# Latents ahead of the context between an HGRN2 and an RG-LRU layer, with the last adaLN block in that gap

## The chip, the cores and the metric

The kernel runs on one core of one Trainium2 chip. The metric is the device time of one execution in microseconds (us), as the median of several runs. The engines are named as the profile names them: PE is TensorE (PEld its weight loads), DVE is VectorE, ACT is ScalarE, POOL is GpSimd, and SP is the queue that issues the transfers of the weights.

## The reference

A backbone of two layers on 512 latent tokens with a prefix of 256 context tokens, 1024 channels. Layer 0 is an HGRN2 mixer (gated linear attention, 16 heads of 128), layer 1 an RG-LRU mixer (convolution of width 4, then a gated recurrence). Cut to the lines that matter here:

```
def reference(x, c, ctx, c_ctx, ada_w, ada_b, norm_g, ...):
    sc = jax.nn.silu(c)
    scc = jax.nn.silu(c_ctx)
    for i in range(DEPTH):
        shift, scale, gate = jnp.split(sc @ ada_w[i] + ada_b[i], 3, axis=-1)
        shift_c, scale_c, gate_c = jnp.split(scc @ ada_w[i] + ada_b[i], 3, axis=-1)
        h = (_rms(x, norm_g[i]) * (1.0 + scale[:, None]) + shift[:, None]).astype(x.dtype)
        hc = (_rms(ctx, norm_g[i]) * (1.0 + scale_c) + shift_c).astype(ctx.dtype)
        ...
            yc, y = hgrn2_mixer(hc, h, hg_w_in[j], lb_all[i], hg_norm_g[j], hg_w_out[j], need_ctx)
        ...
            yc, y = rglru_mixer(hc, h, rg_w_in[j], rg_conv_w[j], rg_conv_b[j], rg_w_a[j], rg_b_a[j], ...)
        x = (x + gate[:, None] * y).astype(x.dtype)
        if need_ctx:
            ctx = (ctx + gate_c * yc).astype(ctx.dtype)
    return _rms(x, final_norm_g).astype(x.dtype)
```

All is float32 to its full precision. [...]

## The kernel before

Channels lie on the 128 partitions, tokens along the free dimension: columns 0 to 255 are the context (segment 0), 256 to 767 the latents (segment 1). The residual stream is one tile `x1` of 8 blocks of 128 channels.

**Products.** `mm3` (L307) issues three matmuls per pair: high by high (L311), high by low of the moving side (L312), low weights by high (L313). A weight tile of 128x1024 comes by a transfer on SP's queue (L114), and `wget` has it split: ACT copies the high part `hi` (L129), DVE subtracts to get `lo` (L130). The raw, `hi` and `lo` tiles rotate through three buffers each, unless `W.slots` gives a weight other tiles.

**The end of layer 0.** `out_item` (L391) multiplies a head's result by its output weights into eight blocks for each segment, tiles `o15_d_i` for the last head, d the block, i the segment; DVE adds each block, times the gate, to `x1` (L405). For head 15, `out_item` does first the context's eight blocks and then the latents' eight, and `sumsq` squares each block as it comes: ACT squares (L285 the first of a group, L288 the others), and the squares are added into three tiles `acc1_0..2` (L289) by POOL for blocks 1 to 3, by DVE for blocks 5 and 6, while block 7 is alone.

**The norm between the layers.** `rstd_of` (L255) sums those tiles over the partitions with matmuls of one column (`msh`, L262), takes a root on ACT (L265) and a reciprocal on DVE (L266), and spreads the result over all partitions with matmuls by an identity (`rbh`, L272), once for each segment.

**The start of layer 1.** `hchunk` (L296) makes one block of `h` for one segment: DVE scales (`scr`, L300), ACT adds the shift and rounds to `h_hi` (L304), DVE forms the rest `h_lo` (L305). Behind each block the first products go: `rc0`, `rc1` (context, 256 columns) and `rl0` to `rl2` (latents, 512 columns) for three weight tiles of the input projection; all context blocks come before the latents' in the code. Then `conv` (L776) evaluates the convolution into `xb` (ACT L789, DVE L792), and `rin(0, 1, 1)` makes the second gate half (tile `r`).

**adaLN.** `ada_block(l, b)` (L224) makes one block of shift, scale or gate: four quarters, each a weight tile and four matmuls with 256 columns (L230), a copy `blk` (L236), four small matmuls that transpose it (`adat`, L240), two additions (L245). Block (1, 5), the last, holds a part of layer 1's gate and is not used in the norm. In `extra(h)` each block of layer 1 is a side generator of a head from 10 to 15; the last one runs in the stretch where heads 14 and 15 are worked on, one quarter beside each second level of the scores (`lv`), `adat` between two products of the input projection.

**Order.** The Tile framework's list scheduler sets the order of the instructions of each engine at compile time, from the order of the code, priorities and its own cost figures; on the chip each engine runs its list in order and waits on semaphores.

## Time and profile before

| what | value |
|---|---|
| time, median of 3 runs | 1581.88 us (1580.87 to 1582.18) |
| the profiled execution's own time | 1581.96 us |
| its span | 1580.2 us |
| PE busy | 1531.5 us, 97% of the span |
| DVE busy | 1207.8 us, 76% |
| ACT busy | 902.6 us, 57% |
| POOL busy | 12.7 us, 1% |

The span is what the profiler shows from the first to the last instruction; the time has 1.8 us around it. PE is busy almost all the time, so the page's totals say little about the place that is changed: some 60 us between the last score products of layer 0 and the steady part of layer 1, from about 1075 to 1133 us. In this stretch PE waits and its granted clock falls.

### The profile page before, as it was taken

Reading aid. Unit: us, or ns where it says so; the run is one execution under the profiler, and the core shown is the slowest. Engines: PE = TensorE matmul, PEld = TensorE weight load, DVE = VectorE, ACT = ScalarE, POOL = GpSimd, SP = SyncE. Lnnn points to the kernel's source line nnn. Section 1 sums busy time; section 2 is a strip of 40 time slices with the busy share of each in tenths; the row PEclk is TensorE's granted clock in tenths of the full one; section 3 lists DMA queues with packets and bytes.
Section 4 is the critical chain, followed back from the end, with each engine's and each line's share of the span. In section 5 each row is a group of like instructions: output and inputs, shape, how many; then the busy total and the mean of one; then the engine's idle time right before and its main releaser. Section 6 shows DMA issues by size and latency. Waiting matters only on the chain.

```text
span 1580.2 us, 34022 instructions
## 1 busy us (share of the span) xinstructions
PE 1531.5 (97%) x14740; PEld 1431.9 (91%) x14740; DVE 1207.8 (76%) x1867; ACT 902.6 (57%) x1423; POOL 12.7 (1%) x16
## 2 busy tenths in 40 slices
PE   5999999999999999999999999998999999999995
PEld 3899999999999999999999999987889988988984
DVE  4767678768867868867876786787768887797888
ACT  4554555555554554554545555654577577667874
POOL 0000000000000000000000000001000000000001
PEclk8999999999999999999999999998999999999996
DMA  8231311110211211223232132202212213222111
GB/s 324 84 121 55 95 55 41 55 55 28 82 41 42 68 41 55 81 68 95 68 95 82 55 108 68 95 15 67 67 54 81 83 51 94 80 77 70 55 53 54
DMA packets 33861, 116.80 MB, mean 74 GB/s; under 512 B 3632, under 2 KB 6064, under 8 KB 33712
## 3 DMA queue, kind: packets, MB, share of 16 engines
q1 hardware_dynamic: 32192, 113.26, 23.0%
q8 instruction: 116, 1.90, 0.5%
q10 hardware_dynamic: 1520, 1.37, 0.3%
q14 instruction: 33, 0.27, 0.1%
HBM read 112.52 MB, written 2.10 MB: 73 GB/s over the span
## 4 chain that ended last, share of the span: by engine, by line
PE 93%; DVE 3%; ACT 2%; issue 1%; POOL 1%; DMA 0%; POOLq 0%; ACTq 0%; DVEq 0%
PE in L311 12%; PE in L312 11%; PE in L313 11%; PE v L381 9%; PE lv L460 4%; PE r L313 4%; PE r L312 4%; PE r L311 4%; PE o L565 4%; PE gt L311 3%; PE gt L312 3%; PE gt L313 3%; PE o L311 3%; PE o L313 3%; PE o L312 3%; PE U L533 2%
## 5 line engine op out<-in xcount | busy, mean ns | idle before, releaser
L311 PE MATMUL in<-h_hi,hi 128*128 128x384 f32 x1024 | 350.6, 343 | 3.4 <-ACT h_hi L304 2.7
L312 PE MATMUL in<-h_lo,hi 128*128 128x384 f32 x1024 | 345.8, 338 | 0.3 <-DVE h_lo L305 0.3
L313 PE MATMUL in<-h_hi,lo 128*128 128x384 f32 x1024 | 344.9, 337 | 0.0
L130 DVE TENSOR_TENSOR lo<-raw,hi 128x1024 fp32r<-128x1024 f32 x160 | 195.2, 1220 | 88.1 <-ACT hi L129 84.7
L129 ACT ACTIVATE hi<-raw 128x1024 fp32r<-128x1024 f32 x160 | 168.2, 1057 | 121.3 <-PE in L312 48.7
L311 PEld LDWEIGHTS in<-h_hi,hi 128*128 128x128 f32 x1024 | 193.1, 189 | 16.8 <-issue 9.9
L312 PEld LDWEIGHTS in<-h_lo,hi 128*128 128x128 f32 x1024 | 193.1, 189 | 2.8 <-issue 1.6
L313 PEld LDWEIGHTS in<-h_hi,lo 128*128 128x128 f32 x1024 | 192.8, 189 | 1.2 <-issue 0.8
L509 DVE TENSOR_TENSOR QQ<-QQ,T 128x768 f32<-128x768 f32 x112 | 117.8, 1052 | 20.8 <-ACT qt L491 20.5
L416 ACT ACTIVATE kt<-KK 128x768 f32<-128x768 f32 x112 | 102.4, 915 | 41.1 <-DVE KK L502 32.7
L502 DVE TENSOR_TENSOR KK<-KK,T 128x768 f32<-128x768 f32 x112 | 117.6, 1050 | 9.7 <-ACT kt L416 8.2
L313 PE MATMUL r<-h_hi,lo 128*128 128x512 f32 (+1 forms) x344 | 123.4, 359 | 0.3 <-DVE lo L130 0.3
L312 PE MATMUL r<-h_lo,hi 128*128 128x512 f32 (+1 forms) x344 | 123.1, 358 | 0.0
L311 PE MATMUL r<-h_hi,hi 128*128 128x512 f32 (+1 forms) x344 | 122.9, 357 | 0.0
L337 ACT ACTIVATE sg<-in 128x384 f32<-128x384 f32 x128 | 61.5, 482 | 99.9 <-PE in L313 99.7
L381 PE MATMUL v<-hi,h_hi 128*128 128x256 f32 x384 | 111.3, 290 | 0.0
L381 PE MATMUL v<-hi,h_lo 128*128 128x256 f32 x384 | 107.4, 280 | 0.0
L381 PE MATMUL v<-lo,h_hi 128*128 128x256 f32 x384 | 107.3, 279 | 0.0
L588 DVE RECIPROCAL sq<-sq 128x384 f32<-128x384 f32 x30 | 76.3, 2545 | 21.1 <-ACT sq L582 20.9
L405 DVE SCALAR_TENSOR_TENSOR x<-o,ada,x 128x256 f32<-128x256 f32 (+1 forms) x184 | 82.3, 488 | 11.3 <-PE o L313 10.6
L311 PE MATMUL o<-rhi,hi 128*128 128x384 f32 (+2 forms) x240 | 85.0, 356 | 1.5 <-DVE lo L130 1.2
L313 PE MATMUL gt<-xh,lo 128*128 128x384 f32 x256 | 86.0, 336 | 0.0
(207 smaller groups left out, 3284.4 us busy)
## 6 DMA issues: line engine op xcount, KB each, us to landing
raw<-in_hgw_dram SPq DMA_DIRECT2D x64, 512.0 KB, 3.7
raw<-in_ada_dram SPq DMA_DIRECT2D x48, 512.0 KB, 4.2
raw<-in_rgi_dram SPq DMA_DIRECT2D x32, 512.0 KB, 3.6
raw<-in_hgv_dram SPq DMA_DIRECT2D x16, 512.0 KB, 3.6
raw<-in_hgo_dram SPq DMA_DIRECT2D x16, 512.0 KB, 3.6
raw<-in_rgg_dram SPq DMA_DIRECT2D x16, 512.0 KB, 3.6
raw<-in_rgo_dram SPq DMA_DIRECT2D x16, 512.0 KB, 3.6
x<-in_x_dram SPq DMA_DIRECT2D x8, 384.0 KB, 5.9
```

Of the source, the lines that this page charges most:

```text
L129: self.nc.scalar.activation(hi, r, AF.Copy)
L130: self.nc.vector.tensor_tensor(lo, r, hi.bitcast(F32), ALU.subtract)
L311: PE.matmul(ps, lhsT=wh, rhs=xh, start=first and i == 0, stop=False, skip_group_check=skip)
L312: PE.matmul(ps, lhsT=wh, rhs=xl, start=False, stop=False, skip_group_check=skip)
L313: PE.matmul(ps, lhsT=wl, rhs=xh, start=False, stop=last and i == n - 1, skip_group_check=skip)
L381: PE.matmul(ps, lhsT=xh[:, kk, t], rhs=w[:, k], start=part == 0 and k == 0 and i == 0 and c % 2 == 0, stop=part == 1 and k == 3 and i == 2 ...
L405: V.scalar_tensor_tensor(xs, ps[:, a - c.start:b - c.start], gate[:, d, 1 - j:2 - j], xs, ALU.mult, ALU.add)
L416: A.activation(view(kt, 0, [[2 * B, n], [B, 2], [1, B]]), view(KK, 0, [[2 * B, n], [NT + B, 2], [1, B]]), AF.Copy)
L460: PE.matmul(ps[w * g:w * g + w, w * c:w * c + w], lhsT=kt[:, o:o + w], rhs=rhs, start=c == 0, stop=c == NC - 1, skip_group_check=True, til ...
L502: V.tensor_tensor(kv, kv, view(T, 1, [[2, n], [m - 1, 2], [0, B]]), ALU.mult)
L509: V.tensor_tensor(qv, qv, view(T, m + 1, [[2, n], [-m - 1, 2], [0, B]]), ALU.mult)
L588: V.reciprocal(rs, rs)
```

## The change

The order between the layers is turned round: the latents' eight output blocks, their norm and their `h` and products come first; the context's output blocks (`out_last(k, 0)`) are written one behind each latent block's products, then come the context's norm, `h` and products. Block (1, 5) of adaLN leaves the head loop; its four quarters go ahead of the latents' norm in the code and its rest (`between`) into the norm, and its weights get tiles of layer 0 that are free by then (`wide`). The first gate half's weights, `rin(0, 1, 0)`, also get two such tiles. `h`'s scratch tile rotates through the pool `ktp` (three buffers) in place of two fixed tiles. `conv` takes the latents first, and for `j = 0` without raised priority.

```
-    def out_item(heads, accs=None, done=None):
+    def out_item(heads):
...
-        parts = segs if accs else halves
-        order = [(d, i) for d in range(DK) for i in range(2)]
-        for d, i in sorted(order, key=lambda x: x[1]) if accs else order:
+        for d, i in [(d, i) for d in range(DK) for i in range(2)]:
...
-            if accs:
-                sumsq(accs, THREE, lambda n: ktp.tile([P, NT], F32, name=n, tag="kt"), d, c)
-                if d == DK - 1:
-                    done(i)
...
+    for j in range(4):
+        W.slots["ada", 1, 5, j] = wide[(0, 1, 5, 1)[j]]
+    W.slots["rin", 0, 1, 0] = (wide[0], wide[1])
...
-        return [ada_block(1, h - 10)] if h >= 10 else []
+        return [ada_block(1, h - 10)] if 10 <= h < NH - 1 else []
...
+    def norm1(i, between=()):
         c = segs[i]
-        rs1.extend(rstd_of([chunks(a, c) for a in accs1], ones_d, f"h1_{i}", ((c.stop - c.start) // P,)))
-
-    run_all(out_item((NH - 1,), accs1, norm1))
+        rs1[i], = rstd_of([chunks(a, c) for a in accs1], ones_d, f"h1_{i}", ((c.stop - c.start) // P,), between)
+    w15 = wget("out", NH - 1)
+
+    def out_last(d, i):
+        e, c = slice(P * d, P * d + P), segs[i]
+        ps = dtile(f"o{NH - 1}_{d}_{i}")[:, :c.stop - c.start]
+        mm3(ps, [(w15[0][:, e], w15[1][:, e], st[NH - 1]["r"][0][:, c], st[NH - 1]["r"][1][:, c])])
+        V.scalar_tensor_tensor(x1[:, d, c], ps, ada[0][:, 2, d, 1 - i:2 - i], x1[:, d, c], ALU.mult, ALU.add)
+        sumsq(accs1, THREE, lambda n: ktp.tile([P, NT], F32, name=n, tag="kt"), d, c)
+
+    for d in range(DK):
+        out_last(d, 1)
+    side = ada_block(1, 5)
+    for _ in range(4):
+        next(side)
+    norm1(1, side)
...
-    first = [[(w, dtile(f"rc{e}")[:, :CTX]) for e, w in enumerate(wx)]]
     wg = wget("rin", 0, 1, 0)
...
-    for i, c in enumerate(segs):
+    first = {1: [(w, (dtile if e < 2 else atile)(f"rl{e}")) for e, w in enumerate(wx + [wg])]}
+    for i in (1, 0):
+        c = segs[i]
         for k in range(DK):
-            hchunk(1, k, i, rs1[i], scr[k % 2])
+            hchunk(1, k, i, rs1[i], ktp.tile([P, NT], F32, name=f"scr1_{i}_{k}", tag="kt"))
             for w, ps in first[i]:
                 mm3(ps, hpairs(w, c, [k]), first=k == 0, last=k == DK - 1)
+            if i:
+                out_last(k, 0)
+        if i:
+            norm1(0)
+            first[0] = [(w, dtile(f"rc{e}")[:, :CTX]) for e, w in enumerate(wx)]
...
-        urgent.enter_context(tc.high_priority(400))
+        if j:
+            urgent.enter_context(tc.high_priority(400))
...
-    for i in range(2):
+    for i in (1, 0):
         for e in range(2):
-            conv(0, e, i, first[i][e][1])
+            conv(0, e, i, first[i][e][1], 0)
```

The list of PE at the latents' norm, before. `msh1_1` is the latents' sum, `rc0` and `rc1` the context's products, `rbh1_1_0` the spread result; a row is line, operation, output<-inputs, size.

```order
L313 MATMUL o15_7_1_13016<-rhi15_12761,lo143_12473 128x512
L262 MATMUL msh1_1_13022<-cst_78,acc1_0_12884 128x1 x4
L311 MATMUL rc0_13051<-h_hi_94,hi144_12889 128x256
L262 MATMUL msh1_1_13022<-cst_78,acc1_1_12885 128x1 x4
L262 MATMUL msh1_1_13022<-cst_78,acc1_2_12886 128x1 x4
L311 MATMUL rc1_13052<-h_hi_94,hi145_13045 128x256
L312 MATMUL rc0_13051<-h_lo_95,hi144_12889 128x256
L313 MATMUL rc0_13051<-h_hi_94,lo144_12890 128x256
L312 MATMUL rc1_13052<-h_lo_95,hi145_13045 128x256
L313 MATMUL rc1_13052<-h_hi_94,lo145_13046 128x256
L311 MATMUL rc0_13051<-h_hi_94,hi144_12889 128x256
L311 MATMUL rc1_13052<-h_hi_94,hi145_13045 128x256
```

The latents' norm stands in a row with the context's products here, which begin ahead of its second sum.

The list of PE at the latents' norm, in the changed kernel, from the last matmul of the latents' outputs to the first of the context's.

```order
L313 MATMUL o15_7_1_12907<-rhi15_12727,lo139_12439 128x512
L262 MATMUL msh1_1_12944<-cst_78,acc1_0_12850 128x1 x4
L240 MATMUL adat1_5_12960<-cst_78,blk1_5_12942 128x2 x4
L262 MATMUL msh1_1_12944<-cst_78,acc1_1_12851 128x1 x4
L262 MATMUL msh1_1_12944<-cst_78,acc1_2_12852 128x1 x4
L272 MATMUL rbh1_1_0_12967<-cst_78,rh1_1_12957 128x128 x4
L311 MATMUL rl0_12986<-h_hi_94,hi144_12934 128x512
L311 MATMUL rl1_12987<-h_hi_94,hi145_12974 128x512
L311 MATMUL rl2_12988<-h_hi_94,hi146_12980 128x512
L311 MATMUL o15_0_0_13002<-rhi15_12727,hi139_12438 128x256
L312 MATMUL rl0_12986<-h_lo_95,hi144_12934 128x512
```

Between the sums now stands `adat` of the adaLN block, and no dense product until `rl0`.

The list of DVE behind the reciprocal of the latents' norm, before.

```order
L266 RECIPROCAL rh1_1_13035<-rh1_1_13035 128x4
L305 SCALAR_TENSOR_TENSOR h_lo_95<-scr1_1_13063,ada1_97,h_hi_94 128x256
L300 SCALAR_TENSOR_TENSOR scr1_0_13062<-x1_81,amul_98,rbh1_0_0_12961 128x256
L300 SCALAR_TENSOR_TENSOR scr1_1_13063<-x1_81,amul_98,rbh1_0_0_12961 128x256
L305 SCALAR_TENSOR_TENSOR h_lo_95<-scr1_0_13062,ada1_97,h_hi_94 128x256
L300 SCALAR_TENSOR_TENSOR scr1_0_13062<-x1_81,amul_98,rbh1_1_0_13038 128x512
L305 SCALAR_TENSOR_TENSOR h_lo_95<-scr1_1_13063,ada1_97,h_hi_94 128x256
L300 SCALAR_TENSOR_TENSOR scr1_0_13062<-x1_81,amul_98,rbh1_0_0_12961 128x256
L300 SCALAR_TENSOR_TENSOR scr1_1_13063<-x1_81,amul_98,rbh1_0_0_12961 128x256
L305 SCALAR_TENSOR_TENSOR h_lo_95<-scr1_0_13062,ada1_97,h_hi_94 128x512
L300 SCALAR_TENSOR_TENSOR scr1_1_13063<-x1_81,amul_98,rbh1_1_0_13038 128x512
L305 SCALAR_TENSOR_TENSOR h_lo_95<-scr1_0_13062,ada1_97,h_hi_94 128x256
```

The blocks of both segments alternate here, and no update of `x1` stands among them.

The list of DVE behind the same reciprocal, in the changed kernel (L735 is the update of `x1` in `out_last`).

```order
L266 RECIPROCAL rh1_1_12957<-rh1_1_12957 128x4
L300 SCALAR_TENSOR_TENSOR scr1_1_0_12989<-x1_81,amul_98,rbh1_1_0_12967 128x512
L300 SCALAR_TENSOR_TENSOR scr1_1_1_13008<-x1_81,amul_98,rbh1_1_0_12967 128x512
L305 SCALAR_TENSOR_TENSOR h_lo_95<-scr1_1_0_12989,ada1_97,h_hi_94 128x512
L305 SCALAR_TENSOR_TENSOR h_lo_95<-scr1_1_1_13008,ada1_97,h_hi_94 128x512
L130 TENSOR_TENSOR lo150_13373<-raw150_13345,hi150_13372 128x1024
L735 SCALAR_TENSOR_TENSOR x1_81<-o15_0_0_13002,ada0_96,x1_81 128x256
L735 SCALAR_TENSOR_TENSOR x1_81<-o15_1_0_13021,ada0_96,x1_81 128x256
L735 SCALAR_TENSOR_TENSOR x1_81<-o15_2_0_13042,ada0_96,x1_81 128x256
L300 SCALAR_TENSOR_TENSOR scr1_1_2_13029<-x1_81,amul_98,rbh1_1_0_12967 128x512
L300 SCALAR_TENSOR_TENSOR scr1_1_3_13050<-x1_81,amul_98,rbh1_1_0_12967 128x512
L735 SCALAR_TENSOR_TENSOR x1_81<-o15_3_0_13063,ada0_96,x1_81 128x256
```

The updates of `x1` for the context's blocks now stand among the latents' blocks: three of them ahead of the third `scr`.

The list of DVE at the end of the latents' blocks, in the changed kernel (L810 is the convolution, L792 before).

```order
L300 SCALAR_TENSOR_TENSOR scr1_1_7_13132<-x1_81,amul_98,rbh1_1_0_12967 128x512
L289 TENSOR_TENSOR acc1_1_12851<-acc1_1_12851,sq6_0_13129 128x256
L130 TENSOR_TENSOR lo147_13307<-raw147_12978,hi147_13306 128x1024
L305 SCALAR_TENSOR_TENSOR h_lo_95<-scr1_1_7_13132,ada1_97,h_hi_94 128x512
L266 RECIPROCAL rh1_0_13158<-rh1_0_13158 128x2
L810 SCALAR_TENSOR_TENSOR xb0_13280<-rl0_12986,prm_76,xb0_13280 128x511
L300 SCALAR_TENSOR_TENSOR scr1_0_0_13166<-x1_81,amul_98,rbh1_0_0_13161 128x256
L300 SCALAR_TENSOR_TENSOR scr1_0_1_13176<-x1_81,amul_98,rbh1_0_0_13161 128x256
L300 SCALAR_TENSOR_TENSOR scr1_0_2_13186<-x1_81,amul_98,rbh1_0_0_13161 128x256
L810 SCALAR_TENSOR_TENSOR xb0_13280<-rl0_12986,prm_76,xb0_13280 128x510
L810 SCALAR_TENSOR_TENSOR xb0_13280<-rl1_12987,prm_76,xb0_13280 128x511
L305 SCALAR_TENSOR_TENSOR h_lo_95<-scr1_0_0_13166,ada1_97,h_hi_94 128x256
```

The context's `scr` and `h_lo` rows come behind the latents' last `h_lo`, with rows of the convolution among them.

## Rows read from the trace of the kernel before

**Rows 1.** The page: first line, and shares of the chain that ended last.

```profile
span 1580.2 us, 34022 instructions
...
PE 93%; DVE 3%; ACT 2%; issue 1%; POOL 1%; DMA 0%; POOLq 0%; ACTq 0%; DVEq 0%
```

**Rows 2.** PE's timeline in head 14: start us, us, engine, line, operation, tiles, count.

```profile
995.63 0.39 PE L230 MATMUL ada<-raw,sc 128*32 128x256 f32 x1
996.22 0.44 PE L311 MATMUL in<-h_hi,hi 128*128 128x384 f32 x1
...
1021.09 0.95 PE L240 MATMUL adat<-cst,blk 128*128 128x2 f32 x8
1021.90 0.42 PE L311 MATMUL in<-h_hi,hi 128*128 128x384 f32 x1
```

**Rows 3.** Windows: length, busy PE, PEld, DVE, ACT, POOL; PEclk, DMA, GB/s.

```profile
1020.00:1030.00 10.00, 10.00 (x63) 10.00 (x62) 9.82 (x15) 6.31 (x8) 0.00 (x0) 1.00 0.19 54
1030.00:1040.00 10.00, 7.85 (x180) 6.56 (x182) 9.95 (x13) 6.89 (x9) 0.00 (x0) 1.00 0.15 50
1076.42:1081.42 5.00, 3.79 (x16) 3.38 (x17) 5.00 (x9) 3.19 (x6) 0.29 (x1) 0.66 0.65 202
1075.42:1133.37 57.95, 50.19 (x242) 42.42 (x241) 47.09 (x78) 31.82 (x53) 7.75 (x6) 0.88 0.21 64
1095.00:1100.00 5.00, 5.00 (x26) 5.00 (x25) 3.19 (x6) 1.02 (x2) 0.00 (x0) 0.50 0.40 129
1105.00:1110.00 5.00, 5.00 (x33) 4.59 (x33) 5.00 (x12) 3.42 (x7) 0.00 (x0) 0.97 0.02 3
```

**Rows 4.** PE's timeline; in brackets the idle time before a row and its releaser.

```profile
1036.85 0.63 PE L460 MATMUL lv<-qt,kt 128*32 128x32 f32 x48 [1.55 <-ACT qt L416]
...
1075.25 0.34 PE L313 MATMUL o<-r,lo 128*128 128x384 f32 x1
1094.78 1.68 PE L262 MATMUL msh<-cst,acc 128*128 128x1 f32 x8 [3.29 <-POOL acc L289]
1108.40 0.28 PE L311 MATMUL rc<-h_hi,hi 128*128 128x256 f32 x1
1108.51 0.28 PE L312 MATMUL rc<-h_lo,hi 128*128 128x256 f32 x1
1133.14 0.40 PE L313 MATMUL r<-h_hi,lo 128*128 128x512 f32 x1
1133.37 0.52 PE L311 MATMUL gt<-xh,hi 128*128 128x384 f32 x2
```

**Rows 5.** The chain between the layers: start us, us, engine, tile, line, count.

```profile
1087.60 0.80 PE msh L262 x8
1096.88 3.21 PE msh L262 x16
1101.79 1.71 PE rbh L272 x8
```

**Rows 6.** Timelines of ACT, POOL and DVE between the layers.

```profile
1085.84 1.06 ACT L129 ACTIVATE hi<-raw 128x1024 fp32r<-128x1024 f32 x1 [1.37 <-DMA raw<-in_rgg_dram]
1104.32 0.72 ACT L304 ACTIVATE h_hi<-scr,ada 128x512 fp32r<-128x512 f32 x1 [2.01 <-DVE scr L300]
...
1089.80 1.30 POOL L289 TENSOR_TENSOR acc<-acc,sq 128x512 f32<-128x512 f32 x1 [5.53 <-ACT sq L288]
...
1078.11 1.12 DVE L604 TENSOR_TENSOR rlo<-gs,rhi 128x512 fp32r<-128x512 f32 x1
1095.59 0.68 DVE L289 TENSOR_TENSOR acc<-acc,sq 128x512 f32<-128x512 f32 x1
1103.53 0.75 DVE L300 SCALAR_TENSOR_TENSOR scr<-x,amul,rbh 128x512 f32<-128x512 f32 x1 [1.11 <-PE rbh L272]
1107.49 0.87 DVE L300 SCALAR_TENSOR_TENSOR scr<-x,amul,rbh 128x256 f32<-128x256 f32 x2
1128.00 4.03 DVE L792 SCALAR_TENSOR_TENSOR xb<-rl,prm,xb 128x511 f32<-128x511 f32 x6
```

More of the change, by code (lines that the diff above doesn't have):

```diff
@@ L389, in v_item @@
                 yield 1300.0
-    def out_item(heads, accs=None, done=None):
+    def out_item(heads):
         ws = [wget("out", h) for h in heads]
         gate = ada[0][:, 2]
-        parts = segs if accs else halves
-        order = [(d, i) for d in range(DK) for i in range(2)]
-        for d, i in sorted(order, key=lambda x: x[1]) if accs else order:
+        for d, i in [(d, i) for d in range(DK) for i in range(2)]:
             e = slice(P * d, P * d + P)
-            c = parts[i]
+            c = halves[i]
             ps = dtile(f"o{heads[0]}_{d}_{i}")[:, :c.stop - c.start]
@@ L723, in build @@
              for i, (pl, t, n) in enumerate(((kdp, "kd", NT), (qp, "q", NT), (sp, "S", 2 * (NC - 1) * P)))]
-    rs1 = []
-    def norm1(i):
+    rs1 = {}
+    def norm1(i, between=()):
         c = segs[i]
-        rs1.extend(rstd_of([chunks(a, c) for a in accs1], ones_d, f"h1_{i}", ((c.stop - c.start) // P,)))
-    run_all(out_item((NH - 1,), accs1, norm1))
+        rs1[i], = rstd_of([chunks(a, c) for a in accs1], ones_d, f"h1_{i}", ((c.stop - c.start) // P,), between)
[12 more added lines that the diff above has]
+    norm1(1, side)
     W.presplit = False
     wx = [wget("rin", 0, 0, e) for e in range(2)]
-    first = [[(w, dtile(f"rc{e}")[:, :CTX]) for e, w in enumerate(wx)]]
     wg = wget("rin", 0, 1, 0)
-    first.append([(w, (dtile if e < 2 else atile)(f"rl{e}")) for e, w in enumerate(wx + [wg])])
-    scr = [ktp.tile([P, NT], F32, name=f"scr1_{k}", tag="kt") for k in range(2)]
-    for i, c in enumerate(segs):
+    first = {1: [(w, (dtile if e < 2 else atile)(f"rl{e}")) for e, w in enumerate(wx + [wg])]}
+    for i in (1, 0):
+        c = segs[i]
         for k in range(DK):
-            hchunk(1, k, i, rs1[i], scr[k % 2])
+            hchunk(1, k, i, rs1[i], ktp.tile([P, NT], F32, name=f"scr1_{i}_{k}", tag="kt"))
             for w, ps in first[i]:
                 mm3(ps, hpairs(w, c, [k]), first=k == 0, last=k == DK - 1)
+            if i:
[3 more added lines that the diff above has]
+            first[0] = [(w, dtile(f"rc{e}")[:, :CTX]) for e, w in enumerate(wx)]
     W.presplit = True
@@ L774, in g_evac, with conv @@
         V.tensor_tensor(s["gs"][:, e], ps, s["gs"][:, e], ALU.mult)
-    def conv(j, e, i, ps):
+    def conv(j, e, i, ps, last=1):
         s = rt[j]
@@ L792, in conv @@
             V.scalar_tensor_tensor(dst, src, cw[:, tap:tap + 1], dst, ALU.mult, ALU.add)
-        if i == 1:
+        if i == last:
             A.activation(s["xh"][:, e], xb, AF.Copy)
```

## The prediction

> **What bounds the kernel now.** I read the page first: the span is 1580.2 us and 93% of the chain that ended last is PE's own work [rows 1]. So the kernel is bound by PE, and the change can only act where PE does not work at its full pace. It touches two such places. I looked at both in tables of windows, which give each engine's busy time in a stretch and the granted clock.
>
> In heads 14 and 15 PE is full in some windows, but from 1020 to 1040 it is DVE that has 9.82 and 9.95 of each 10 us, while PE sinks to 7.85 [rows 3]. Work taken from PE is worth its length in the first sort of window, and little in the second.
>
> Between the layers the stretch from 1075.42, where PE is done with the last output matmul of heads 12 to 14 (a step of 0.17 behind its start, [rows 4]), to 1133.37, where layer 1's first `gt` matmul starts [rows 4], takes 57.95 us, with PE busy for 50.19 of it and a mean granted clock of 0.88 [rows 3]. The matmuls in it need far less at full pace. One step from matmul to matmul is 0.23 us for 512 columns and 0.115 for 256 [rows 4]. Head 15's outputs (24 of each size) are 8.4 us, `rc` (48 of 256) 5.6, `rl` (72 of 512) 16.8, the second gate half `r` (24 of 512) 5.6, and the small matmuls of the two norms some 4.9 by the full-pace step of 0.1 us each (0.80 for x8, [rows 5]). That is 41.3 us, so 16.6 are lost, 7.8 by standing still and the rest by the clock: PE waits 3.29 us for POOL's sums, then the small sums take 1.68 for x8, twice as long as 0.80 before [rows 4, 5], and the window at 1095 shows 0.50, the lower level of 1.2 GHz, although PE counts as busy for all of it [rows 3]. Once `rc` has run, 1105 to 1110 shows 0.97 again, nearly all 2.4 GHz [rows 3]. The question is thus how much the new order loses of this stretch.
>
> **The change, part by part.**
>
> *Head 14's relief.* One quarter of the adaLN block holds PE from 995.63 to 996.22 [rows 2]; of these 0.59 us I count 0.55, since its first matmuls lie beside the last of `lv`. Four quarters are 2.2 us. `adat` is 0.81 (1021.09 to 1021.90, [rows 2]), but stands where DVE has no slack [rows 3], so I give it nothing; the two small additions that leave DVE there are worth some 0.2. I take -2.4. Bounds: 0, if DVE's pace hides all of it, and -3.1 with `adat`.
>
> *What PE does first in the gap.* Three quarters of the moved block come directly behind 1075.42: 3 x 0.59 = 1.8, until 1077.2. They cost little, because the latents' low part `rlo` is ready only at 1079.23 (1078.11 + 1.12, [rows 6]), and only the first three output matmuls can run without it. From 1079.25 come 21 matmuls of 512 columns, 4.9 us; the fourth quarter, 0.6; and 0.7 for a lower clock at first, as in before, where the same five microseconds show a mean of 0.66 [rows 3] (an estimate: two of those microseconds at the lower level, less what the waits cover). That makes 1085.45.
>
> *The sums.* POOL's three additions now wait for squares that ACT makes behind the adaLN copy and behind a weight split whose data arrive late (in before that split waited for its transfer until 1085.84, [rows 6]; the transfer is issued earlier now, and I take 1084.1, by an estimate from the order on SP). Then the split's 1.06 and a square end at 1085.8, and two additions of 1.30 [rows 6] end at 1088.5. PE stands still for 3.05 us. If the transfer comes no earlier, all that follows is up to 1.7 later.
>
> *The latents' norm.* Here the new order has a longer chain and nothing beside it: sum 0, `adat`, the adaLN additions and one of 0.68 to `acc1_1` [rows 6] on DVE, sums 1 and 2, root, reciprocal, spread, `scr` 0.75, `h_hi` 0.72 [rows 6]. In before the context's `rc` matmuls stood among these; now nothing dense does. With the sums 1.6 us for 16, `adat` 0.85 and spread 0.9 at full pace it ends at about 1096.1. At the lower level the sums 1 and 2 are 3.21 and the spread 1.71 [rows 5], `adat` twice 0.85: about 1099.6. Which? A pause of 1.55 us at 1036.85 left the matmuls behind it at full pace, one of 3.29 did not [rows 4]. The estimated 3.05 is nearest to the second, and small matmuls did not bring the clock back in before. I take 1099.6, with sum 0 at full pace, and keep 1096.1 as the other bound.
>
> The Trainium skill, page "TensorE: Matmul & The Clock Gate", section "Why this matters for your kernels", warns against idle gaps between bursts of matmuls, since TensorE then falls to half clock. The row of 3.29 agrees, and it is the rule that speaks against this change; by it the sum is the one with the lower level, +5.5 below, and by the row of 1.55 alone it would be about 0.
>
> *The latents' products.* PE's work here is `rl` 16.8, the context's outputs 2.8 and its norm sums and spread 1.8, together 21.4. Three waits are new. The third `scr` stands on DVE behind three updates of `x1` which themselves wait for matmuls between the first blocks' products: about 1.0. The context's second sum waits for ACT's square and DVE's addition, both behind weight splits: about 1.5. The last `h_lo` behind a split: 0.2. With a rest of 0.4 this is 24.5 us at full pace; with the lower level for the first 4.5 us (in before it lasted about as long into `rc`, [rows 3]) 26.65. The end is 1126.2.
>
> *The context's blocks.* Their `scr` and `h_lo` all come last now, and DVE sets the pace: 16 operations of 0.40 (0.87 for two, [rows 6]) are 6.4, and four rows of the convolution among them, 0.66 each (4.03 for six, [rows 6]), 2.6. With 0.9 until the first `h` is there, 9.9 us for `rc`, whose matmuls need 5.6. The 4.3 us between could be filled by matmuls of `rin(0, 1, 1)`, whose split weights are ready early now, but the list has only two of them among `rc`'s. Bounds: 5.6 and 9.9. The end is 1136.1.
>
> *The rest of the gate half.* 22 x 0.23 = 5.1: 1141.2. In before `gt` started at 1133.37. So the stretch is 7.9 us longer, of which the quarters and `adat` make about 3 and the rest is the context's tail.
>
> *Taken at nothing:* the slots for `rin(0, 1, 0)` (the split that they let go ahead lies beside `rl`'s matmuls; uncovered it is 1.06 on ACT, [rows 6], and about as much on DVE), and the convolution's lost priority (its result is needed only by `gt`, behind 22 + 24 matmuls). Uncovered, the convolution costs the 4.03 of its six rows. POOL's additions and everything in heads 0 to 13 stay.
>
> **The sum.** +7.9 - 2.4 = +5.5 on the profiled execution's 1581.96: 1587.5. That execution lies 0.08 above the median of 1581.88, so no correction is due.
>
> **Rivals.**
>
> *The clock stays up.* If PE's pause is a little shorter than 3.05, the chain ends at 1096.1 and the products take 24.5: 1135.6, +2.2 - 2.4 = about 0, some 1582. For it: the estimate is only just under the row of 3.29, and three quarters of adaLN and `adat` fill PE. Against: before `adat` PE has only one-column matmuls, and those ran at 0.50 in before [rows 3]. It decides whether PE's pause there is like the row of 1.55 or like that of 3.29.
>
> *Faster: the waits in line vanish.* DVE's list is in an order that need not bind. If the context's blocks keep up with PE, `rc` takes 6.5 in place of 9.9, the waits of 1.0 and 1.5 in the latents' products go, and the clock stays up: 1135.6 - 3.4 - 2.5 = 1129.7, -3.7, with -2.4 about -6; without the second of these about -5: 1577. For it: the old order left 16.6 us to be had, and PE has 72 matmuls of 512 columns behind which six microseconds of context work could hide. Against: the lists put the context's DVE rows behind the last `h_lo` of the latents. It decides where `rl` starts before 1096 and `rc` takes under 7 us.
>
> *Worse: a second fall.* `rc` at 57% of PE's time, in pieces behind DVE, comes after sums of one column for the context. If the clock falls there again, `rc`, `r` and the next matmuls run at half for some 4 us: +2; with the late transfer (+1.7) and head 14's relief at 0 (+2.4) the sum is +11.6, 1593.5.
>
> *The change does nothing:* head 14's gain hidden by DVE and the gap equal; 1582, counted under the first rival.
>
> **How the numbers follow.** A measurement of this kernel tells about 0.2%, 3.2 us, from no change. My forecast, the lower level in the norm and the slow tail, 1585 to 1591: 0.47. Clock up or gains that cancel, 1579 to 1585: 0.23. Faster than 1578.7: 0.20. Worse than 1591: 0.10. So faster 0.20, same 0.23, slower 0.57. The range leaves out about half of the faster case and the top of the worst: 1578.5 to 1593.5. The forecast's own range is 1585 to 1591, from the transfer (1.7), head 14 (2.4 up, 0.7 down) and the tail.
>
> **What would show it.** Head 14: the profile has no `ada` rows there, and `gt`'s start in layer 1 moves by about +5.5 as a whole. Gap: `msh` of the latents begins some 3 us behind the last `o`, at a clock of 0.50 in the window that follows; `rl` starts 24 us behind 1075.42 (less the 2.4); PE has idle time put down to DVE `h_lo` in `rc`, about 4 us; `rc` ends some 37 us behind the first `rl`. I am wrong if the granted clock is 1.00 through the norm, if `rl` starts within 20 us of the gap's start, or if `rc` takes less than 7 us.

## The result, and the profile after

The changed kernel takes 1594.25 us (median of 5 runs, 1593.61 to 1595.69), the kernel before 1581.88 in the same comparison: a ratio of 1.0085 (95% interval 1.0073 to 1.0097; the quotient of the two medians, 1.0078, lies in it). It is 12.4 us slower, where 5.5 were forecast and 1593.5 was the upper end of the range.

The stretch between the layers, from the end of the last output matmul of heads 12 to 14 to the first `gt`, shows it. PE's timeline of the changed kernel, with the idle time before a row and its releaser in brackets:

```profile
1074.84 1.50 PE L230 MATMUL ada<-raw,sc 128*32 128x256 f32 x24
1077.12 0.96 PE L311 MATMUL o<-rhi,hi 128*128 128x512 f32 x3 [0.78 <-ACT rhi L597]
...
1080.23 0.62 PE L230 MATMUL ada<-raw,sc 128*32 128x256 f32 x2
...
1082.38 0.62 PE L230 MATMUL ada<-raw,sc 128*32 128x256 f32 x2
...
1083.82 0.62 PE L230 MATMUL ada<-raw,sc 128*32 128x256 f32 x4
...
1089.36 1.87 PE L262 MATMUL msh<-cst,acc 128*128 128x1 f32 x8 [3.32 <-POOL acc L289]
1091.09 1.85 PE L240 MATMUL adat<-cst,blk 128*128 128x2 f32 x8
1093.80 3.58 PE L262 MATMUL msh<-cst,acc 128*128 128x1 f32 x16 [0.86 <-DVE acc L289]
1097.94 2.07 PE L272 MATMUL rbh<-cst,rh 128*128 128x128 f32 x8 [0.57 <-DVE rh L266]
1101.68 1.65 PE L311 MATMUL rl<-h_hi,hi 128*128 128x512 f32 x3 [1.66 <-ACT h_hi L304]
...
1125.21 1.05 PE L262 MATMUL msh<-cst,acc 128*128 128x1 f32 x8 [1.45 <-DVE acc L289]
...
1128.03 0.63 PE L312 MATMUL rl<-h_lo,hi 128*128 128x512 f32 x1
1128.46 0.63 PE L313 MATMUL rl<-h_hi,lo 128*128 128x512 f32 x1
...
1129.74 0.86 PE L272 MATMUL rbh<-cst,rh 128*128 128x128 f32 x4
1132.36 0.51 PE L311 MATMUL rc<-h_hi,hi 128*128 128x256 f32 x2 [1.76 <-ACT h_hi L304]
1133.67 0.58 PE L312 MATMUL rc<-h_lo,hi 128*128 128x256 f32 x1 [0.80 <-DVE h_lo L305]
...
1147.04 0.51 PE L311 MATMUL gt<-xh,hi 128*128 128x384 f32 x2
```

The stretch ran from 1075.42 to 1133.37 before [rows 4]. Now it runs from 1074.74 to 1147.04. Two pauses are to be seen, each with small matmuls behind it. The first is 3.32 us ahead of the latents' first sum; then sums, `adat` and spread follow one on another, with waits of 0.86, 0.57 and 1.66 between, until `rl` starts at 1101.68. The second is at the context's norm: 1.45, 1.76 and 0.80. From 1127 on `rl`'s matmuls of 512 columns are 0.43 apart, not 0.23 (1128.03, 1128.46).

Windows of the changed kernel (length, busy time of PE, PEld, DVE, ACT and POOL, PE's granted clock, DMA share, GB/s):

```profile
1074.74:1147.04 72.30, 59.49 (x285) 47.62 (x284) 49.37 (x82) 32.46 (x55) 6.46 (x6) 0.83 0.21 66
...
1090.00:1095.00 5.00, 4.14 (x20) 4.05 (x20) 1.98 (x4) 0.00 (x0) 0.00 (x0) 0.50 0.00 0
...
1100.00:1105.00 5.00, 3.34 (x9) 2.70 (x9) 4.04 (x5) 2.33 (x3) 0.00 (x0) 0.50 0.00 0
...
1125.00:1130.00 5.00, 4.79 (x19) 3.79 (x20) 2.78 (x5) 2.44 (x5) 0.00 (x0) 0.69 0.33 105
...
1135.00:1140.00 5.00, 5.00 (x34) 4.94 (x34) 5.00 (x12) 2.05 (x5) 0.00 (x0) 0.79 0.00 0
```

The whole stretch is 72.30 us, 14.35 longer than before [rows 3]. PE stands still for 12.81 of it (7.76 before) and has a mean granted clock of 0.83 (0.88 before). The clock is at 0.50, the level of 1.2 GHz, from 1090 to 1105. It falls again behind the second pause, 0.69 and 0.79 in the windows at 1125 and 1135. In the window at 1090 PE counts as busy for 4.14 of 5 us, yet with small matmuls only.

What became of head 14's relief? Two landmarks lie around it that both kernels have: the last `adat` of block (1, 4), and the last output matmul of heads 12 to 14, which starts at 1075.25 before [rows 4]. The `adat` matmuls from 900 to 1000 us (the last number of the times is the start of the last one), before and then in the changed kernel, and the last output matmul there:

```profile
L240 PE MATMUL adat<-cst,blk x16: 166/251/251, 914.2 to 980.8; 128*128 128x2 f32 x16
L240 PE MATMUL adat<-cst,blk x16: 166/251/251, 913.4 to 980.0; 128*128 128x2 f32 x16
```

```profile
1074.57 0.34 PE L313 MATMUL o<-r,lo 128*128 128x384 f32 x1
```

Between these landmarks lie 94.4 us before and 94.6 now: nothing was gained. The traces of the experiments below agree: with the block in the heads the distance is 94.4 to 94.7, without it 94.5 to 94.7 in six kernels and 96.1 in four. What PE waited for longest in heads 14 and 15, before and then in the changed kernel (us in total, times, longest):

```profile
PE lv L460 <- ACT qt L416: 2.5, 2, 1.6
```

```profile
PE lv L454 <- ACT qt L485: 1.3, 1, 1.3
PE o L311 <- ACT r L597: 1.1, 1, 1.1
```

Before, all PE's waits from 940 to 1075.4 add up to 3.1 us, now to 4.8. So 1.7 of the 2.2 us that the quarters left are seen again as waits for ACT and DVE.

### The profile page after: what moved, and what is told of

It is laid out like the page before. It is cut to its first block, busy times and chain, and to the rows that moved or that the text cites. A ratio compares the mean times of both kernels' runs of the same rounds, so it can differ in the third digit from the quotient of the medians.

```text
span 1592.5 us, 34020 instructions
## 1 busy us (share of the span) xinstructions
PE 1536.5 (96%) x14740; PEld 1434.0 (90%) x14740; DVE 1207.8 (76%) x1867; ACT 902.2 (57%) x1423; POOL 11.4 (1%) x16
## 4 chain that ended last, share of the span: by engine, by line
PE 91%; DVE 4%; ACT 3%; issue 1%; POOL 0%; DMA 0%; POOLq 0%; ACTq 0%; DVEq 0%
PE in L311 11%; PE in L312 11%; PE in L313 11%; PE v L381 9%; PE r L313 4%; PE r L312 4%; PE r L311 4%; PE lv L454 4%; PE o L559 4%; PE gt L311 3%; PE gt L312 3%; PE gt L313 3%; PE o L311 3%; PE o L312 3%; PE o L313 3%; PE U L527 2%
## 5 line engine op out<-in xcount | busy, mean ns | idle before, releaser
L311 PE MATMUL gt<-xh,hi 128*128 128x384 f32 x256 | 85.5, 337 | 0.3 <-ACT xh L812 0.3
```

The lines of the kernel that those rows point to most:

```text
L311: PE.matmul(ps, lhsT=wh, rhs=xh, start=first and i == 0, stop=False, skip_group_check=skip)
```

## The experiments

Each kernel was timed beside the kernel before. The ratio with its 95% interval is to the kernel before of the same comparison, whose median was 1580.78 to 1581.88. The last column gives the stretch between the layers in the kept trace, with the time of the run that was traced; where that lies far from the median, the trace need not be typical.

| kernel | median, us | ratio to before | stretch, us (run traced) |
|---|---|---|---|
| kernel before | 1581.88 | 1 | 57.95 (1581.96) |
| changed kernel | 1594.25 | 1.0085 (1.0073 to 1.0097) | 72.30 (1594.25) |
| e1_block_back | 1591.59 | 1.0062 (1.0048 to 1.0076) | 69.05 (1591.59) |
| e2_block_only | 1581.12 | 0.9998 (0.9989 to 1.0007) | 59.32 (1581.56) |
| e3_ctx_fill | 1587.31 | 1.0038 (1.0025 to 1.0050) | 65.42 (1589.60) |
| e8_split_only | 1581.35 | 1.0000 (0.9991 to 1.0009) | 60.81 (1580.39) |
| e4_hold_after | 1589.11 | 1.0046 (1.0034 to 1.0059) | 65.15 (1587.56) |
| e6_hold_before | 1580.34 | 0.9993 (0.9984 to 1.0003) | 59.93 (1582.81) |
| e7_rest_late | 1591.62 | 1.0065 (1.0052 to 1.0077) | 68.98 (1590.37) |
| e5_mix | 1584.65 | 1.0026 (1.0014 to 1.0038) | 63.28 (1588.53) |
| e9_hold_all | 1581.06 | 1.0002 (0.9993 to 1.0010) | 61.88 (1584.95) |
| e10_hold_both | 1588.68 | 1.0049 (1.0037 to 1.0061) | 63.88 (1588.70) |
| e11_hold_back | 1586.89 | 1.0034 (1.0022 to 1.0046) | 63.36 (1587.21) |
| e12_mix_hold | 1579.59 | 0.9995 (0.9987 to 1.0004) | 56.71 (1581.83) |
| e13_mix_late | 1577.60 | 0.9976 (0.9966 to 0.9985) | 54.62 (1577.01) |
| e14_mix_no_added | 1582.86 | 1.0007 (0.9998 to 1.0016) | 57.14 (1579.84) |
| e15_mix_back | 1577.87 | 0.9979 (0.9967 to 0.9990) | 60.54 (1583.05) |

**The block.** Put back in the heads, with the new order kept:

```
-    side = ada_block(1, 5)
-    for _ in range(4):
-        next(side)
-    norm1(1, side)
+    norm1(1)
```

> The changed kernel with adaLN block (1, 5) back in the loop over the heads, and with the new order of latents and context kept. Theory A (the loss is PE's clock: between the layers PE stands still and then has only small sums, twice, and the lower clock costs more than the block): both falls of the clock stay; the chain of the latents' norm loses adat (1.85 us) and the wait of 0.86 behind it, some 1 us of quarters leave the outputs, and 0.7 comes back in head 14: 1594.2 - 3 = about 1591. Rival B (the block itself is the loss: it cost its whole length between the layers and gave only 0.7 us back in head 14): most of the 12.4 us goes, 1582 to 1585. Rival C (the loss is the order of DVE's rows: the context's blocks last): 1592 to 1594.

Its quarters left where they are, and only `adat` and the additions moved behind the fourth latent block's products:

```
-    norm1(1, side)
+    norm1(1)
...
                 out_last(k, 0)
+                if k == 3:
+                    run_all(side)
```

> The changed kernel with adat and the adaLN additions behind the fourth latent block's products, the quarters where they are. Theory A: the chain of the norm loses adat's 1.85 us and 0.86 of the wait behind it: 1591.5, as with the whole block back in the heads, which says that the quarters cost nothing in the gap. If the quarters cost their length too, the time is still 1 to 2 us above that, 1593.

Both come to 1591.6, so the quarters cost nothing that can be measured. They lie in waits: in e1, without the block, PE waits 3.2 us for `rhi` ahead of the latents' outputs, with it 0.8. What costs is `adat` in the chain of the norm, some 3 us (2.6 by the medians, 3.3 by the stretches). Rival B falls: about three quarters of the loss remain without the block. Rival C, the order of DVE's rows, gave 1592 to 1594 for e1, too near to what was measured to tell.

The kernel before with the block alone moved, ahead of and into the latents' norm:

```
+        side = ada_block(1, 5) if i else ()
+        for _ in range(4 * i):
+            next(side)
-        rs1.extend(rstd_of([chunks(a, c) for a in accs1], ones_d, f"h1_{i}", ((c.stop - c.start) // P,)))
+        rs1.extend(rstd_of([chunks(a, c) for a in accs1], ones_d, f"h1_{i}", ((c.stop - c.start) // P,), side))
```

> The kernel before with only the adaLN block moved: its four quarters stand on PE between the last latents' output and the first sum of the latents' norm, adat behind that sum; context first as before. Theory A: the quarters (2.0 us) lie in the pause of 3.29 us, the pause that is left is about 1.3 us, the clock stays up through the sums and the context's first products; 4 to 5 us of half clock go, 0.7 us of head 14 too, adat and its additions cost 1 to 2: about 1579, granted clock 1.00 from 1090 to 1105. Rival B: 1584 to 1586, since the block costs its length (2.0 + 0.85 + the additions, less 0.7). Rival C: no change, 1581 to 1583.

No change. Of the three only rival C had that, but the trace shows another reason. PE's timeline and windows of this kernel:

```profile
1092.51 1.93 PE L230 MATMUL ada<-raw,sc 128*32 128x256 f32 x32
1094.78 1.05 PE L262 MATMUL msh<-cst,acc 128*128 128x1 f32 x8 [0.33 <-POOL acc L289]
1096.44 1.19 PE L240 MATMUL adat<-cst,blk 128*128 128x2 f32 x8 [0.61 <-ACT blk L236]
...
1097.85 3.41 PE L262 MATMUL msh<-cst,acc 128*128 128x1 f32 x16
```

```profile
1092.00:1096.00 4.00, 3.49 (x43) 2.04 (x41) 3.98 (x5) 4.00 (x7) 2.56 (x2) 1.00 0.00 0
1096.00:1100.00 4.00, 3.56 (x20) 3.56 (x21) 2.02 (x6) 0.90 (x2) 0.00 (x0) 0.65 0.42 131
1100.00:1104.00 4.00, 3.98 (x18) 3.71 (x19) 2.41 (x6) 1.17 (x3) 0.00 (x0) 0.50 0.00 0
```

The quarters filled the pause, and only 0.33 us of 3.29 was left of it. The clock fell all the same, during the sums: 1.00, 0.65, 0.50. So my theory was too narrow: no pause above 0.61 us was needed. What stood ahead of the fall were the quarters' 32 matmuls in 128x32 positions, eight sums and `adat`; which of them let the clock fall, the quarters among them, this run doesn't tell.

**The order alone.** The kernel before with only the two tiles for `rin(0, 1, 0)`:

```
+    W.slots["rin", 0, 1, 0] = (wide[0], wide[1])
```

> The kernel before with only the two tiles of layer 0 for the split weights of rin(0, 1, 0), so that the split of rin(0, 1, 1) need not wait for the last product of rl (4.10 us of ACT's time). Theories A, B and C: PE waited only 0.31 us for this, 1581.5 to 1582. Rival D (the split's wait held back more than PE's row shows, since DVE and ACT stood still behind it): 1578 to 1580.

Nothing, and rival D falls. The changed kernel with the context's outputs ahead of the latents' norm:

```
+    for d in range(DK):
+        out_last(d, 0)
     norm1(1, side)
...
-            if i:
-                out_last(k, 0)
```

> The changed kernel with head 15's context outputs written ahead of the latents' norm instead of one behind each latent block. Theory A: 2.8 us of dense matmuls now lie in the pause of 3.32 us, and the context's squares and additions are done long before its norm, so that the second pause (1.45 us) and the second fall of the clock, 1127 to 1137, go: about 1587. If the first fall stays (the sums remain small matmuls alone) the gain is about 4 us, 1590; if it goes too, 1585. Rival B: within 1.5 us of 1594, since the block stays where it is. Rival C: the three updates of x1 ahead of the third block go (1.0 us), the context's tail stays: 1592 to 1593.

1587.3, the number that theory A gave, but not by its way. PE's wait ahead of the first sum is 0.7 us in place of 3.3, and none is left ahead of the context's sums. The first fall of the clock stays (0.50 through the sums, until about 1108), and for that case theory A had 1590. The second fall isn't gone either: 0.60 from 1128 to 1132. Rival C alone, with 1592 to 1593, gave too little.

**The clock.** Matmuls of 512 columns whose result goes unused, put behind each group of sums by a forced order (`dense(n, prev)` issues n of them behind `prev`; the counts stand for the places ahead of the first sum, behind each of three groups, behind the spread):

```
-    norm1(1, side)
+    norm1(1, side, busy((13, 4, 2, 4, 6)))
```

> The changed kernel with matmuls of 512 columns added that compute nothing used: 13 in the pause before the first sum of the latents' norm, 4, 2 and 4 behind its three groups of sums, 6 behind the spread of the result (29, 6.8 us at full pace, most of it in waits). Theory A (the clock falls because nothing but small matmuls and waits stands there): the granted clock stays 1.00 to the first rl; the sums, adat and the spread go from 9.4 to about 5 us, rl loses its slow start (2.2), the added matmuls cost about 1.5 where they lie in no wait: 1588 to 1590. Rival B (the adaLN block's length) and rival C (DVE's order): no gain, 1594 to 1596, by the added matmuls. The second fall, at the context's norm, is left as it is.

PE's timeline of this kernel:

```profile
1086.20 3.14 PE L745 MATMUL busy<-rhi 128*128 128x512 f32 x13
1089.18 0.95 PE L272 MATMUL msh<-cst,acc 128*128 128x1 f32 x8
...
1094.19 0.95 PE L240 MATMUL adat<-cst,blk 128*128 128x2 f32 x8
...
1097.80 0.97 PE L326 MATMUL rl<-h_hi,hi 128*128 128x512 f32 x3 [0.28 <-ACT h_hi L319]
```

Eight records of sums take 0.95 us and not 1.87, `adat` 0.95 and not 1.85, and `rl` starts 22.7 us behind the start of the stretch and not 26.9. Its windows show 1.00 to 1120; the second fall stays (0.50 from 1124 to 1128). That is 5.1 us on the medians, with 29 useless matmuls in it, as theory A had it.

The same in the kernel before, at the latents' norm and then at every place where PE waits:

```
+                           busy((13, 2, 2, 4, 0)) if i else None))
```

```
+                           busy((13, 2, 2, 4, 0) if i else (6, 0, 0, 0, 0))))
+    dense(8, LAST[0], NH - 2)
```

> The kernel before with such matmuls added at the latents' norm: 13 in the pause of 3.29 us and 2, 2 and 4 behind the three groups of sums (21). Theory A with the clock set by the small sums as well as by the pause (moving the adaLN block into the pause closed it to 0.33 us and the clock fell all the same, during the sums): 1.00 from 1090 to 1105, of 10.4 us at the lower level 5 come back, the matmuls outside the pause cost 1 to 2: 1577 to 1578.5. Rival (that stretch is bound by DVE and ACT, so a faster PE only waits): 1580 to 1583.

> The kernel before with added dense matmuls (512 columns, result unused) at every place between the layers where PE waits or has small sums alone: 8 ahead of head 15's outputs, 6 ahead of the context's first sum, then as in the run that held the clock at the latents' norm (13, 2, 2, 4). In that run the clock fell earlier instead, from 1084 to 1093. Theory A: 1.00 from 1076 to 1133, the 10 us that PE had at the lower level give 4 to 5 back, 1577. Rival (DVE and ACT set the pace there): 1580 to 1582.

Both miss: no gain clear of the noise. In the profile of e6 the clock holds at the norm, but is at 0.51 from 1084 to 1092, under head 15's outputs. In that of e9 it falls at the norm after all. The window of e6, then two of e9:

```profile
1084.00:1092.00 8.00, 7.98 (x27) 6.88 (x28) 2.91 (x7) 1.47 (x4) 0.00 (x0) 0.51 0.22 66
```

```profile
1096.00:1100.00 4.00, 3.69 (x25) 3.03 (x23) 4.00 (x7) 2.49 (x5) 0.33 (x1) 1.00 0.35 94
1100.00:1104.00 4.00, 4.00 (x15) 3.59 (x15) 1.82 (x5) 0.26 (x1) 0.00 (x0) 0.50 0.54 161
```

Neither trace is typical. That of e6 is of the longest of its 11 runs, which lie between 1576.56 (with a mean granted clock of 0.992, against 0.988 in the run traced) and 1582.81; so one run had what was expected. That of e9 is of one of three runs near 1584.5 with 0.988; its nine others have 0.991 to 0.993, more than the 0.984 to 0.988 of the kernel before beside it, and take 1579.09 to 1581.78. With the clock better kept, 35 added matmuls in it, the kernel before thus gained 2.3 us at most. Both medians also lie where the rival had them (DVE and ACT set the pace there), and these runs don't set it apart from the length of the added matmuls. I did not settle why the same counts (13, 2, 2, 4) held the clock in one trace and not in the other.

Both norms of the changed kernel filled, without and then with the block back in the heads:

```
-            norm1(0)
+            norm1(0, (), busy((2, 0, 5, 4, 8)))
```

> The changed kernel with added dense matmuls at both norms: the latents' as in the first such run (13, 4, 2, 4, 6), and at the context's 2, 5, 4 and 8 around the sums and behind the spread. What the clock cost the changed kernel is 1594.2 less this time (and the added matmuls' own 1 to 2 us); what is then left above the kernel before with its clock held is due to the order and to the block. Theory A with the clock as the whole loss: within 3 us of that kernel. Theory A with clock and waits each about half: 1586 to 1587.5, some 9 or 10 us above it.

> The same with the adaLN block back in the loop over the heads and 8 added matmuls in the wait ahead of the latents' outputs. The block at a full clock: if it costs only adat and the wait for its additions (0.85 + 0.86, less what head 14 gives back), this is 1 to 2 us faster than the run with the block; with theory B 4 us or more faster.

One window of e10 over the whole stretch:

```profile
1076.00:1140.00 64.00, 60.39 (x331) 47.69 (x330) 47.57 (x82) 32.62 (x54) 7.22 (x6) 1.00 0.23 74
```

With the clock at 1.00 throughout it takes 1588.7, no less than e4, so the second norm's 19 added matmuls cost what the clock gave there. It still stands 7.3 us above the kernel before, more than either form of theory A gave. The clock is thus not the whole loss. What is left I put down to the chains of the two norms, in which PE has nothing of use to do, whether it waits or is kept warm: 48 added matmuls of 0.23 us are 11 us, and 3.6 us of waits remain. No run changed the order of DVE's rows alone, but e10's trace bounds rival C, with the clock up:

```profile
1127.42 0.40 PE L326 MATMUL rc<-h_hi,hi 128*128 128x256 f32 x2
...
1130.00 0.50 PE L326 MATMUL rc<-h_hi,hi 128*128 128x256 f32 x2 [0.88 <-ACT h_hi L319]
```

Eight added matmuls, 1.9 us, stand between the context's spread and `rc`, and `rc` waits 0.88; two waits in the latents' products, at the third block and for an update of `x1`, are 0.8 and 0.2. So by what PE waits in these places DVE's order has at most some 3.8 of the 7.3; what the added matmuls around the sums may hide isn't in that. The medians give the block 1.8 of it (e11), as forecast; but e11 has 8 more added matmuls, and in its trace the clock falls once more (0.68 from 1092 to 1096), so this isn't the block's price at a full clock.

**The order, with work among the sums.** Four context blocks ahead of the first sum, one behind each group, one behind the spread; the context's norm, `h` and products among the latents' blocks:

```
+    for d in range(4):
+        out_last(d, 0)
+    def ctx(s, prev):
+        if s in (1, 2, 3):
+            with behind(prev):
+                out_last(3 + s, 0)
...
+    for k in range(DK):
+        chunk(1, k)
+        if k == 2:
+            run_all(side)
+            norm1(0)
...
+        if k > 3:
+            chunk(0, k - 4)
```

> The changed kernel's idea with dense work among the small sums: latents' outputs and the quarters of the block first, then four context output blocks ahead of the latents' first sum and one behind each group of sums and one behind the last, so that the context's 2.8 us of matmuls stand where only sums stood; adat and the context's norm behind the third latent block; the context's h and products among the latents' from the fifth block on, so that no context tail is left. Theory A: the first fall of the clock goes or is cut to half (2 to 4 us), adat's 2.7 us leave the chain, the context's tail with its waits (2.9) and its fall (1.5) goes: 1594.2 - 12 to 15 = 1579 to 1582. Theory C alone (DVE's order is the loss, the clock is not): 1586 to 1588. Rival B: 1590 or more, since the block stays between the layers.

Better by some 9 us than the changed kernel, yet short of the forecast of theory A, and better than theory C alone gave: the clock falls during the sums, and the list put `adat` and the context's sums between the first latent products, so that it stays at 0.50 to 1115 in the run traced (3.9 us above the median). With added matmuls, and with the context's norm behind the fifth latent block and its `h` from the seventh on:

```
+        return dense((10, 2, 2, 4, 7)[s], prev)
```

> The version with the context's outputs among the latents' sums and the context's h and products among the latents' (1584.65), with added dense matmuls (10, 2, 2, 4, 7) where the sums and waits of the latents' norm still let the clock fall from 1091 to 1114, and the context's products from the seventh block on. Theory A: the 23 us at the lower level hold some 17 us of matmuls, of which half comes back, less 2 for the added ones: 1577 to 1579, faster than both kernels. Theory C (DVE's rows set the pace): 1583 to 1585.

PE's timeline of this kernel:

```profile
1091.89 0.95 PE L272 MATMUL msh<-cst,acc 128*128 128x1 f32 x8
...
1101.80 0.95 PE L240 MATMUL adat<-cst,blk 128*128 128x2 f32 x8
1102.61 1.48 PE L272 MATMUL msh<-cst,acc 128*128 128x1 f32 x12
...
1105.24 0.63 PE L328 MATMUL rl<-h_hi,lo 128*128 128x512 f32 x1
```

1579.6, near the forecast of theory A and well below that of theory C (1583 to 1585), but not apart from the kernel before. Two faults are to be seen. The first sum waits for the 10 added matmuls until 1091.89, and POOL was done at 1089.3. And `adat` and the context's sums still stand ahead of the rest of the first products; behind them, from 1105.24, a matmul of 512 columns takes 0.63. Both mended (e13), then with all five counts at 0 (e14), then with the first counts and the block back in the heads (e15):

```
-        return dense((10, 2, 2, 4, 7)[s], prev)
+        prev = dense((0, 5, 2, 4, 7)[s], prev)
...
+        if k == 2:
+            with behind(LAST[0]):
+                run_all(side)
+        if k == 4:
+            norm1(0, (), lambda s, prev: prev)
```

> The version with the context's work among the latents' and added dense matmuls (1579.59), with three faults that its trace shows mended: the 10 matmuls ahead of the first sum go (POOL was done at 1089.32 and PE computed nothing used until 1091.89; 5 stand behind that sum instead, ahead of the context block that waits for x1), and adat and the context's norm stand behind the third and fifth latent block by a forced order, so that 2.4 us of small matmuls no longer come between the first three products, where the clock fell from 1104.95 to 1108.4. If the order of latents first is no loss in itself: 1579.6 - 2 - 1.6 = 1576, faster than the kernel before. If it is one (DVE's rows set the pace behind the norm): 1579 to 1581.

> The same without any added matmul, so that only real work stands between the sums. If the clock needs dense work there, the context's outputs (0.35 us each) are too little and it falls for the norm and the first latent blocks as in the first such version: 1580 to 1582. If they are enough: 1576, as with the added ones.

> The same as the first of these three, with the adaLN block back in the loop over the heads. The block's cost between the layers when adat lies among dense products: its first three quarters lie in the wait for the latents' rhi and rlo, the fourth costs 1.6 us in three pieces, adat 0.9, less 0.7 of head 14: 1.5 to 2 us faster than with the block there. If the quarters lie all in waits: the same within 0.7.

One window of e13 from 1076 to its first `gt`, two of e14 and two of e15:

```profile
1076.00:1129.06 53.06, 50.53 (x278) 40.91 (x275) 46.60 (x81) 30.95 (x51) 6.81 (x6) 1.00 0.26 89
```

```profile
1092.00:1096.00 4.00, 3.98 (x21) 3.68 (x19) 1.67 (x5) 1.79 (x4) 1.20 (x2) 0.52 0.00 0
1096.00:1100.00 4.00, 2.16 (x8) 1.67 (x8) 4.00 (x7) 2.51 (x6) 0.00 (x0) 0.50 0.37 117
```

```profile
1088.00:1092.00 4.00, 4.00 (x18) 3.52 (x18) 2.49 (x6) 1.62 (x4) 1.45 (x2) 0.59 0.18 72
1092.00:1096.00 4.00, 4.00 (x20) 3.81 (x18) 0.77 (x2) 0.00 (x0) 0.00 (x0) 0.50 0.00 0
```

e13 holds 1.00 throughout, and its stretch is 54.6 us against 57.95 before. At 1577.6 it beats both kernels, the kernel before by 0.24%; its 9 runs (to 1579.42) all lie below the 21 of the kernel before (from 1579.68). Without the 18 added matmuls the clock falls to 0.52 and 0.50 at the norm: the context's outputs of 0.35 us each don't hold it. That loses 5.3 us on the medians; the trace, of a run 3.0 below the median, shows 2.5 of it in the stretch, and where the rest lies isn't shown. With the block in the heads the median is the same within 0.3 us, so among dense products the block costs nothing between the layers, as it gains nothing in head 14. But e15 has the same added matmuls as e13 and doesn't always hold the clock: five of its 7 runs take 1576.53 to 1577.96 with a mean granted clock of 0.989 to 0.991, and two take 1583.05 and 1583.07 with 0.985. One of those two was traced, and its windows fall to 0.59 and 0.50.

## Why the prediction was wrong

The direction and the place were right, and so was the first half of the mechanism: a pause ahead of the latents' sums, with the lower clock behind it. Four terms of the sum were mis-sized. Two of them were wrong in their step too: the relief, where a wait came in the place of the work, and the tail, where PE did not wait for DVE as counted and ran at the lower level instead.

- *Head 14's relief*, taken at -2.4: measured +0.1. The prediction's own bound of 0 is what came. It saw that DVE sets the pace behind 1020, and still counted the quarters ahead of it, where PE is full, at their length. PE's waits grew by 1.7 instead.
- *The latents' norm*, 24.2 us from the start of the stretch to `rl`: measured 26.9. About 1.1 of the 2.7 come with the outputs: the fourth quarter was counted at 0.6, and the list issues it in three pieces that take 0.62 each. The pause is 3.32 for the 3.05 forecast, a size that came near by other events than those counted. Another 0.9 is the first sum, taken at full pace and run at half. POOL was late for a reason that I had half right, as the chain of the changed kernel shows. ACT's split (1084.98) did not wait for its transfer, but stood behind the copy of the adaLN block, which waited for the fourth quarter:

```profile
1083.88 0.58 PE ada L230 x4
...
1084.49 0.03 ACT blk L236
...
1084.98 0.60 ACT hi L129
...
1085.93 0.63 ACT sq L288
...
1086.69 1.28 POOL acc L289
```

- *The latents' products*, 26.65: measured 28.06, from 1101.68 to 1129.74. The wait at the context's sums came as forecast (1.45 for 1.5). The one at the third block was 0.79 for 1.0. New is the second fall of the clock, which made the last block's six matmuls 0.43 us apart and not 0.23.
- *The context's blocks*, 9.9: measured 11.5, to 1141.2. The prediction had DVE set the pace here, with about 4 us in which PE waits for `h_lo`. The trace has one such wait, of 0.80. Behind it `rc`'s matmuls follow one another without a wait, to 1137 at the lower level, 0.21 us apart, and from there 0.12 apart. With the clock up, in e10, `rc` takes 7.5 us (1127.42 to 1134.92) with one wait of 0.88. So it was luck that the size came near. The second fall stood as a rival at +2, in a case with a chance of 0.10; it is part of the result, and by its rows it costs some 3 us (six matmuls of `rl` at 0.2 more, about 20 of `rc` at 0.1 more).

With these four, 2.5 + 2.7 + 1.4 + 1.6, and 0.7 for three matmuls of the next gate half that now stand ahead of `gt`, the forecast of 5.5 becomes 14.4; the profiled execution was 0.8 ahead before it came to head 14, which makes the 13.7 by which `gt` starts later. The span is 12.3 longer: 0.7 of the rest are those three matmuls, and 0.7 I did not trace. (In the prediction's sum, 1141.2 less 1133.37 is 7.8 and not 7.9.)

The rival in which the clock stays up was wrong for this kernel (0.50 for 15 us), and so was its condition: a shorter pause isn't enough, as e2 shows. Its estimate of about 1582 looks too low as well, for e10 has the clock up and takes 1588.7; but 11 us of added matmuls are in that, so no run measures it cleanly. The faster rival asked for what e13 does: clock up, waits in line gone, the context's blocks kept up with PE. It gave 1577, and e13 takes 1577.6; that they meet is luck in part, since the rival counted 2.4 us of head 14 that never came, and e13 has another order and 18 added matmuls. The order of latents first is no loss in itself: with the context's work among the latents' it takes as long as the kernel before (e14), and less when the clock is held (e13). What lost was that its sums and its context tail stood alone; how the tail's part divides between the clock and DVE's order is bounded by e10 and not measured.

The rule of the Trainium skill that was cited, page "TensorE: Matmul & The Clock Gate", section "Why this matters for your kernels", says that idle gaps between bursts of matmuls bring half clock. The trace agrees with its direction (3.32 us idle, then 0.50); e2 shows that closing the gap was not enough here.

## What to carry to other kernels

A busy PE need not be a warm one: where a chain of one-column sums, transposes and broadcasts stands alone, look at the granted clock and not at the busy share, and put dense work between its links, not only into its pause; then time it over many runs, because the clock may hold in some and fall in others. Work that is taken off PE where another engine is a little behind gains nothing, so measure from one landmark to the next instead of counting its length. And turning an order round moves the bare chain to the other part: here there had to be dense work at both norms before the new order paid.

## What the runs showed of the hardware

The clock fell with PE nearly without a pause (0.33 and 0.61 us) behind the quarters' matmuls, sums and `adat` (e2: 0.65, then 0.50). At the latents' norm it stayed at 1.00 in the traces of e4 and e13, where two to five dense matmuls stood between the sums; it fell in that of e9, with two, and in that of e15, with the counts of e13. So added matmuls made it likelier that the clock held, and did not secure it. One and the same kernel can take both ways from run to run: e15's 7 runs are five up to 1577.96 and two near 1583.06, with mean granted clocks of 0.989 to 0.991 and of 0.985. Page "TensorE: Matmul & The Clock Gate" of the Trainium skill, section "Part 1: The HAM clock gate", says of a kernel's start that its number of slow matmuls varies from run to run with the phase in which the start meets the gate; the two ways of e15 are alike in kind, in the middle of a kernel, and no run here shows the phase itself. And the matmuls of the adaLN block cost by the piece: 24 records in a row took 1.50 us, the fourth quarter's 8, in three pieces between other matmuls, 0.62 each time.
